# Local attention of a hybrid decoder step in plain fp32, on 64x64 and 128x64 tiles of the array

## The chip, the cores and the metric

The kernel runs on one core of one Trainium2 chip, as one launch. The metric is the device time of an execution in microseconds (us), as the median of several runs. The core's engines are named as the profile names them: PE (TensorE, matmuls; PEld is its weight load), DVE (VectorE), ACT (ScalarE), POOL (GpSimd) and SP (SyncE, which issues DMAs).

## What is computed

One layer of a decoder trunk for 1024 prompt tokens and 8 single-token samples. Ten projections of the normalised input feed two branches: retention (4 heads) and local attention (16 query heads of width 64 in 4 groups, one key/value head per group, a window of 128 keys, a learned sink per head). The branches are gated, projected, merged and projected once more. The change is in the local attention of the prompt alone, which is this part of the reference:

```python
def sink_attention(q, k, v, allowed, sinks):
    s = jnp.einsum('bnqhgd,bnkhd->bnhgqk', q.astype(jnp.float32), k.astype(jnp.float32)) * (SWA_HD ** -0.5)
    s = jnp.where(allowed[None, :, None, None], s, -jnp.inf)
    sink = jnp.broadcast_to(sinks.astype(jnp.float32)[None, None, :, :, None, None], s.shape[:-1] + (1,))
    p = jax.nn.softmax(jnp.concatenate([s, sink], axis=-1), axis=-1)[..., :-1]
    return jnp.einsum('bnhgqk,bnkhd->bnqhgd', p, v.astype(jnp.float32))

def swa_prompt(q, k, v, sinks):
    ...
    i = jnp.arange(SWA_BLOCK)[:, None]
    j = jnp.arange(2 * SWA_BLOCK)[None, :]
    d = i + SWA_BLOCK - j
    band = (d >= 0) & (d < WINDOW)
    ...
    o = sink_attention(qb, with_prev(kb), with_prev(vb), allowed, sinks)
```

A query at place i of a block of 128 sees keys i+1 to 127 of the block before and 0 to i of its own: 128 keys in all.

## The kernel before

**Stages.** Phase 1 first normalises and transposes the input. Then it goes through eight groups of work, four of retention and four of local attention (one per key/value head, `g`). The stretch from 416 to 900 us of the span holds the local attention. Phases 2 and 3, the projections of the branches and the output, follow. The large projections, lines 211 to 213 and 221 to 223, run in all stages. Each multiplies fp32 data that was split into a high and a low part of type fp32r, by three matmuls (high by high, high by low, low by high).

**One block of local attention** is `swa_tile(g, t)`, for t = 0 to 7, 32 in all; block 0 of a group has no block before it. It is a generator with five steps. First comes a projection to 384 columns (256 of queries for 4 heads, 64 of keys, 64 of values, `acc`), then the norm and rotary work on DVE, ACT and POOL. In step two, queries (`qr`, line 512) and keys (`kd`, line 513, the 64 columns twice) are transposed on PE. The queries are then stored as `qs` with the high part in partitions 0 to 63 and the low part in 64 to 127 (lines 517 and 518). The keys go into `kThi` and `kTlo`, each twice over the partitions. In step three, lines 533 and 534, each head has one matmul with `kThi` and one with `kTlo`, over 256 keys (128 in block 0). Since the weights `qs` hold both parts, two matmuls give the sum of all products. DVE then puts the keys of the block before over those that the mask forbids (line 536), takes the maximum (538), and ACT takes the exponential (487). So 128 probabilities per query are left, stored as in a ring. In step four the probabilities are transposed (545) and split into `pThi` and `pTlo` (lines 138 and 139), and four selects on POOL (554) make of them the part that belongs to the block before (`pHp`, `pLp`) and the part of the own block. In step five four matmuls (565, 566; two in block 0) of 512 columns, 4 heads of 128 queries, multiply these by values `vv`, high part in columns 0 to 63 and low in 64 to 127. Lines 568 and 572 add the two halves and store them in `oT`.

**Order.** `groups` writes a list of steps: a block's own next step, steps of the two blocks before it, and between them steps of gates and merge gates (`gate_block`, `mg_block`), which are projections and serve as filling. A scheduler of the framework then sets the order of instructions on each engine by a timeline of its own. Each engine runs its own list in order. Score tiles come from a pool of two PSUM buffers (`psc`), weighted sums from one (`pav`).

**Other fp32 matmuls of the kernel before.** Lines 442, 610 and 624 multiply plain fp32 data, without parts, on column tiles of the array that are 32 wide (`tile_position=(0, 32 * i)`). They serve the 8 samples. An fp32 matmul stands as two rows in the trace, an fp32r matmul as one.

Of the kernel before, what the change touches and what calls it, by code (L numbers as in the profile page):

```python
# [18 lines left out]
P = 128  # L19
D = 1024  # L20
SEQ = 1024
# [7 lines left out]
SH, KVH, G, HD = 16, 4, 4, 64  # L29
# [45 lines left out]
def shape_constants():  # L75
# [17 lines left out]
    i = np.arange(P)[:, None]  # L93
    j = np.arange(P)[None, :]
    out["c_band"] = (j > i) * 1.0
    misc = np.zeros((P, NMISC))
    for h in range(RH):
# [24 lines left out]
class Body:  # L122
# [370 lines left out]
    def swa_tile(self, g, t, units, st, oT):  # L493
        nc = self.nc
        acc = self.t(self.pacc, [P, 512], "acc")
        self.gemm_tok(acc[:, :384], units, self.hhi, self.hlo, t)
        qr, kd, rs = self.swa_rope(acc[:, :384], t)
        vv = self.t(self.ap, [P, 2, HD], "vv", F32R, bufs=4)
        self.copy_hi_lo(vv[:, 0, :], vv[:, 1, :], acc[:, 320:384], nc.vector)
        if t == NT - 1:  # L500
            vf = self.t(self.ap, [P, HD], "vf", bufs=1)
            nc.scalar.activation(out=vf[:], in_=acc[:, 320:384], func=AF.Copy)
            nc.sync.dma_start(out=self.o["kp"][0, 0, :, g, :], in_=kd[:, 0, :])
            nc.sync.dma_start(out=self.o["vp"][0, 0, :, g, :], in_=vf[:])
        vprev, st["v"] = st["v"], vv
        yield
        if t == 0:
            st["k"] = (self.t(self.ap, [P, SEQ], "kThi", F32R, bufs=1), self.t(self.ap, [P, SEQ], "kTlo", F32R, bufs=1))
# [12 lines left out]
        self.copy_hi_lo(khi[:, ks], klo[:, ks], pt[:, 2, :], nc.vector)  # L521
        yield
        k0 = (t - 1) * P if t else 0
        nk = 2 * P if t else P
        s = self.t(self.ap, [P, G, P], "s", bufs=2)
        mx = self.t(self.sm, [P, 4], "mx", bufs=2)
        two = lambda x: x.unsqueeze(1).broadcast_to([P, 2, P])
        scs = []
        for i in range(2):
            sc = self.t(self.psc, [P, 2, 256], "sc")  # L530
            for a in range(2):
                j = 2 * i + a
                nc.tensor.matmul(sc[:, a, :nk], qs[:, i, a, :], khi[:, k0 : k0 + nk], start=True, stop=False)  # L533
                nc.tensor.matmul(sc[:, a, :nk], qs[:, i, a, :], klo[:, k0 : k0 + nk], start=False, stop=True)  # L534
            cur = sc[:, :, nk - P : nk]
            nc.vector.copy_predicated(
                out=cur, mask=two(self.after[:].bitcast(U32)), data=sc[:, :, 0:P] if t else two(self.neg[:]))
            nc.vector.tensor_reduce(out=mx[:, 2 * i : 2 * i + 2], in_=cur, axis=AX.X, op=ALU.max)
            scs += [sc[:, a, nk - P : nk] for a in range(2)]
# [6 lines left out]
        big = lambda x: x[:].rearrange("p (j n) -> p j n", j=G)  # L546
        new = lambda nm: self.t(self.ap, [P, 512], nm, F32R, bufs=2 if "T" in nm else 1)
        hi, lo = new("pThi"), new("pTlo")
        self.copy_hi_lo(hi[:], lo[:], pt[:].rearrange("p a b -> p (a b)"), nc.vector)
        pT = [(hi, lo)]  # L550
        if t:
            hp, lp = new("pHp"), new("pLp")
            for dst, src, sign in ((hp, hi, 1), (lp, lo, 1), (hi, hi, -1), (lo, lo, -1)):
                nc.gpsimd.affine_select(
                    out=big(dst), in_=big(src).bitcast(F32), compare_op=ALU.is_ge, fill=0.0,
                    base=-1 if sign > 0 else 0, pattern=[[0, G], [-sign, P]], channel_multiplier=sign)
            hc, lc = hi, lo
            pT = [(hp, lp), (hc, lc)]
        nblk = len(pT)
        yield  # L560
        vs = [vprev, vv] if nblk == 2 else [vv]
        po = self.t(self.pav, [P, 512], "av")
        for blk in range(nblk):
            w = vs[blk][:].rearrange("p a b -> p (a b)")
            nc.tensor.matmul(po[:], w, pT[blk][0][:], start=(blk == 0), stop=False)  # L565
            nc.tensor.matmul(po[:], w, pT[blk][1][:], start=False, stop=(blk == nblk - 1))  # L566
        bot = self.t(self.ap, [HD, 512], "rbig", bufs=1)
        nc.scalar.activation(out=bot[:], in_=po[HD:P, :], func=AF.Copy)
        b4 = bot[:].rearrange("p (i a n) -> p i a n", i=2, a=2)
        p4 = po[0:HD, :].rearrange("p (i a n) -> p i a n", i=2, a=2)  # L570
        for a in range(2):
            nc.vector.tensor_tensor(out=oT[a * HD : (a + 1) * HD, :, ks], in0=p4[:, :, a, :], in1=b4[:, :, a, :], op=ALU.add)

    def swa_rows(self, g, units, oT):
        nc = self.nc
# [283 lines left out]
    def swa_consts(self):  # L859
# [6 lines left out]
        self.after = self.t(ap, [P, P], "band")  # L866
        nc.sync.dma_start(out=self.after[:], in_=self.i["c_band"][:])
        self.neg = self.t(ap, [P, P], "neg")
        nc.gpsimd.memset(self.neg[:], NEG)
        self.sink = self.t(ap, [P, SH], "sink")  # L870
        nc.sync.dma_start(out=self.sink[:], in_=self.i["swa_sinks"][0:1, :].broadcast_to([P, SH]))
        self.nsink = self.t(ap, [P, SH], "nsink")
# [135 lines left out]
```

## Time and profile before

| | us |
|---|---|
| runs | 1172.18, 1173.7, 1174.65 |
| median of the 3 runs | 1173.7 |
| the profiled execution, its own time | 1171.8 |
| span of its trace | 1170.0 |
| PE busy | 1148.1 |
| DVE busy | 638.6 |
| ACT busy | 436.8 |
| POOL busy | 428.3 |

The profile is one execution. Spans start at the core's first instruction. A matmul's duration in the trace overlaps that of the next one, so a row's cost is read as the distance from its start to the next row's start. A form such as 128*32 in a PE row gives the array's rows and columns that are used, and 128x256 the output's partitions or rows and columns.

### The profile page before, as it was taken

How to read it: one execution, taken by the hardware profiler on the slowest of the kernel's cores; microseconds unless marked ns; L12 is line 12 of the kernel's file. 1: busy time of each engine (PE TensorE's matmuls, PEld its weight loads, DVE VectorE, ACT ScalarE, POOL GpSimd, SP SyncE). 2: the span in 40 equal slices, each digit the busy share in tenths (PEclk: the TensorE clock that was granted, in tenths of full speed). 3: DMA queues.
4: the chain of work that ended last, by engine and by line, in shares of the span. 5: the costliest groups of instructions: out<-in, count | busy, mean ns of one | idle time of the engine just before them, and what ended most of it. 6: DMA issues, size and time to landing. Idle time of an engine off the chain costs nothing.

```text
span 1170.0 us, 19270 instructions
## 1 busy us (share of the span) xinstructions
PE 1148.1 (98%) x7140; PEld 1095.1 (94%) x7140; DVE 638.6 (55%) x1818; ACT 436.8 (37%) x1130; POOL 428.3 (37%) x398
## 2 busy tenths in 40 slices
PE   6999999999999999999999999999999999999998
PEld 5899999999999999999999999999999999999876
DVE  5854545555543487767766766678634312564121
ACT  6543342343344244544453455345534201221010
POOL 5434025216225435634463446345742211221010
PEclk9999999999999999999999999999999999999999
DMA  9224115314123411311141114102437744544221
GB/s 321 61 81 123 51 40 184 97 43 126 37 63 104 140 32 59 107 43 32 33 138 38 33 33 138 38 16 74 140 132 227 232 149 148 166 129 136 82 91 64
DMA packets 125165, 116.51 MB, mean 100 GB/s; under 512 B 17608, under 2 KB 113224, under 8 KB 125040
## 3 DMA queue, kind: packets, MB, share of 16 engines
q1 hardware_dynamic: 118160, 106.83, 29.6%
q10 hardware_dynamic: 6912, 8.46, 2.0%
q8 instruction: 56, 0.92, 0.3%
q14 instruction: 37, 0.30, 0.1%
HBM read 84.88 MB, written 32.44 MB: 100 GB/s over the span
## 4 chain that ended last, share of the span: by engine, by line
PE 90%; DVE 3%; DMA 2%; issue 2%; POOL 1%; ACT 1%; SPq 0%; ACTq 0%; POOLq 0%; DVEq 0%
PE acc L211 16%; PE acc L212 15%; PE acc L213 15%; PE acc L221 10%; PE acc L223 10%; PE acc L222 10%; PE acc L231 1%; PE acc L232 1%; PE sc L533 1%; PE sc L534 1%; PE av L565 1%; PE av L566 1%; PE tr L545 1%; DMA oT<-d_o 1%; POOL wlo L168 1%
## 5 line engine op out<-in xcount | busy, mean ns | idle before, releaser
L168 POOL TENSOR_TENSOR wlo<-wraw,whi 128x1024 fp32r<-128x1024 f32 (+1 forms) x92 | 205.5, 2240 | 303.7 <-ACT whi L167 260.4
L211 PE MATMUL acc<-hhi,whi 128*128 128x344 f32 x864 | 279.8, 324 | 1.5 <-ACT tg L297 1.5
L212 PE MATMUL acc<-hlo,whi 128*128 128x344 f32 x864 | 277.6, 321 | 0.0
L213 PE MATMUL acc<-hhi,wlo 128*128 128x344 f32 x864 | 277.3, 321 | 0.0
L221 PE MATMUL acc<-whi,hhi 128*128 128x384 f32 x512 | 175.5, 343 | 2.5 <-ACT hhi L138 1.2
L223 PE MATMUL acc<-whi,hlo 128*128 128x384 f32 x512 | 174.5, 341 | 0.0
L222 PE MATMUL acc<-wlo,hhi 128*128 128x384 f32 x512 | 174.5, 341 | 0.0
L211 PEld LDWEIGHTS acc<-hhi,whi 128*128 128x128 f32 x864 | 162.5, 188 | 4.6 <-ACT tg L297 2.2
L212 PEld LDWEIGHTS acc<-hlo,whi 128*128 128x128 f32 x864 | 162.4, 188 | 1.3
L213 PEld LDWEIGHTS acc<-hhi,wlo 128*128 128x128 f32 x864 | 162.4, 188 | 1.2 <-POOL wlo L168 0.2
L167 ACT ACTIVATE whi<-wraw 128x1024 fp32r<-128x1024 f32 (+1 forms) x92 | 90.3, 984 | 173.5 <-PE acc L212 110.0
L146 POOL TENSOR_TENSOR rs<-ms,nhalf 128x1 f32<-128x1 f32 (+3 forms) x81 | 68.5, 848 | 206.6 <-DVE ms L145 205.7
L221 PEld LDWEIGHTS acc<-whi,hhi 128*128 128x128 f32 x512 | 97.0, 190 | 4.8 <-ACT hhi L138 1.6
L222 PEld LDWEIGHTS acc<-wlo,hhi 128*128 128x128 f32 x512 | 97.0, 189 | 0.5 <-issue 0.2
L223 PEld LDWEIGHTS acc<-whi,hlo 128*128 128x128 f32 x512 | 96.9, 189 | 0.5 <-DVE hlo L139 0.2
L287 POOL TENSOR_TENSOR oT<-oT,tg 128x344 f32<-128x344 f32 x48 | 48.3, 1007 | 64.7 <-DVE tg L285 54.4
L487 ACT ACTIVATE s<-sc,ng,rs 128x128 f32<-128x128 f32 x128 | 56.9, 455 | 22.9 <-DVE ng L484 22.6
L223 PE MATMUL acc<-whi,mlo 128*128 128x512 f32 x128 | 50.5, 395 | 0.0
L222 PE MATMUL acc<-wlo,mhi 128*128 128x512 f32 x128 | 50.3, 393 | 0.0
L221 PE MATMUL acc<-whi,mhi 128*128 128x512 f32 x128 | 50.1, 393 | 0.0
L975 DVE TENSOR_TENSOR x<-acc,x 128x512 f32<-128x512 f32 x16 | 11.0, 690 | 68.7 <-PE acc L223 63.8
L285 DVE SCALAR_TENSOR_TENSOR tg<-tg,acc 128x344 f32<-128x344 f32 x48 | 24.5, 510 | 31.4 <-ACT tg L284 31.1
(361 smaller groups left out, 2372.9 us busy)
## 6 DMA issues: line engine op xcount, KB each, us to landing
wraw<-in_w_in SPq DMA_DIRECT2D x36, 512.0 KB
d_t<-tg ACTq DMA_DIRECT2D x48, 172.0 KB
d_o<-oT SPq DMA_DIRECT2D x16, 516.0 KB
tt<-d_t SPq DMA_DIRECT2D x48, 172.0 KB
wraw<-in_w_in SPq DMA_DIRECT2D x32, 256.0 KB
st<-d_o SPq DMA_DIRECT2D x9, 516.0 KB
d_m<-tt SPq DMA_DIRECT2D x24, 172.0 KB
mm<-d_m SPq DMA_DIRECT2D x24, 172.0 KB
```

The costliest lines, as they stand in the source:

```text
L146: nc.gpsimd.tensor_tensor(out=rs[:p, :width], in0=ms[:p, :width], in1=self.nhalf[:p, :width], op=ALU.pow)
L167: nc.scalar.activation(out=hi[:, :f], in_=raw[:, :f], func=AF.Copy)
L168: nc.gpsimd.tensor_tensor(out=lo[:, :f], in0=raw[:, :f], in1=hi[:, :f].bitcast(F32), op=ALU.subtract)
L211: nc.tensor.matmul(ps, whi[:, k, :], hi[:, cs], start=(k == 0), stop=False)
L212: nc.tensor.matmul(ps, whi[:, k, :], lo[:, cs], start=False, stop=False)
L213: nc.tensor.matmul(ps, wlo[:, k, :], hi[:, cs], start=False, stop=(k == KT - 1))
L221: nc.tensor.matmul(ps, hi[:, k, a:b], whi[:, kk, :], start=(k == 0), stop=False)
L222: nc.tensor.matmul(ps, hi[:, k, a:b], wlo[:, kk, :], start=False, stop=False)
L223: nc.tensor.matmul(ps, lo[:, k, a:b], whi[:, kk, :], start=False, stop=(k == KT - 1))
L285: nc.vector.scalar_tensor_tensor(out=tg[:], in0=tg[:], scalar=1.0, in1=ps[:, :BL], op0=ALU.add, op1=ALU.mult)
L287: nc.gpsimd.tensor_tensor(out=sl, in0=sl, in1=tg[:], op=ALU.mult)
L487: nc.scalar.activation(out=s[:p, j, :], in_=src[j], func=AF.Exp, bias=ng[:p, j : j + 1], scale=scale[j], accum_out=l[:p, j : j + 1])
```

## The change

The local attention of the prompt no longer splits its operands: queries, keys, probabilities and values stay fp32, and each product is one fp32 matmul. The scores are made in four 64x64 tiles of the array: two halves of its rows for two heads (`a`) by two halves of its columns for the two halves of the queries of a block (`e`). A half of 64 queries needs 192 keys (64 or 128 in block 0). The two heads' scores now stand in two PSUM tiles, each in a bank of its own. The mask shrinks to 64 columns. The probabilities are copied once (`pA`, on ACT). Four selects on POOL over 64 partitions and 256 elements zero one triangle in each half and write the other into `pB`, whose upper half stays zero. The weighted sums run in two column halves, on 128x64 tiles: `pA` with one order of the values and `pB` with the other. For that, POOL keeps a second copy of the values with the partition halves exchanged (`vv[:, 1]`). In block 0 both matmuls use the first column half and `pB` is not used.

```diff
@@ swa_tile
-        vv = self.t(self.ap, [P, 2, HD], "vv", F32R, bufs=4)
-        self.copy_hi_lo(vv[:, 0, :], vv[:, 1, :], acc[:, 320:384], nc.vector)
+        vv = self.t(self.ap, [P, 2, HD], "vv", bufs=4)
+        nc.scalar.activation(out=vv[:, 0, :], in_=acc[:, 320:384], func=AF.Copy)
+        for e in range(2):
+            nc.gpsimd.tensor_copy(out=vv[(1 - e) * HD : (2 - e) * HD, 1, :], in_=vv[e * HD : (e + 1) * HD, 0, :])
...
-        qs = self.t(self.ap, [P, 2, 2, P], "qs", F32R, bufs=2)
-        for a in range(2):
-            src = pt[a * HD : (a + 1) * HD, 0:2, :]
-            nc.scalar.activation(out=qs[0:HD, :, a, :], in_=src, func=AF.Copy)
-            nc.vector.tensor_tensor(out=qs[HD:P, :, a, :], in0=src, in1=qs[0:HD, :, a, :].bitcast(F32), op=ALU.subtract)
-        khi, klo = kT
+        qs = self.t(self.ap, [P, 2, P], "qs", bufs=2)
         ks = slice(t * P, (t + 1) * P)
-        self.copy_hi_lo(khi[:, ks], klo[:, ks], pt[:, 2, :], nc.vector)
+        nc.scalar.activation(out=qs[:], in_=pt[:, 0:2, :], func=AF.Copy)
+        nc.vector.tensor_copy(out=kT[:, ks], in_=pt[:, 2, :])
...
         for i in range(2):
-            sc = self.t(self.psc, [P, 2, 256], "sc")
             for a in range(2):
-                j = 2 * i + a
-                nc.tensor.matmul(sc[:, a, :nk], qs[:, i, a, :], khi[:, k0 : k0 + nk], start=True, stop=False)
-                nc.tensor.matmul(sc[:, a, :nk], qs[:, i, a, :], klo[:, k0 : k0 + nk], start=False, stop=True)
+                pa = slice(a * HD, (a + 1) * HD)
+                for e in range(2):
+                    k1 = t * P + (e + 1) * HD
+                    nc.tensor.matmul(
+                        sc[a][e * HD : (e + 1) * HD, i, lo[e] : 3 * HD], qs[pa, i, e * HD : (e + 1) * HD], kT[pa, k1 - 3 * HD + lo[e] : k1],
+                        start=True, stop=True, tile_position=(a * HD, e * HD))
...
-        hi, lo = new("pThi"), new("pTlo")
-        self.copy_hi_lo(hi[:], lo[:], pt[:].rearrange("p a b -> p (a b)"), nc.vector)
-        pT = [(hi, lo)]
+        pA = self.t(self.ap, [P, G, 2, HD], "pA", bufs=2)
+        nc.scalar.activation(out=pA[:].rearrange("p j e n -> p (j e n)"), in_=pt[:].rearrange("p a b -> p (a b)"), func=AF.Copy)
+        pB = self.pB[t % 2]
         if t:
...
+            for dst in (pB, pA):
+                for e in range(2):
+                    old = (dst is pA) == (e == 0)
+                    sign = 1 if old else -1
+                    nc.gpsimd.affine_select(
+                        out=dst[HD:P, :, e, :], in_=pA[HD:P, :, e, :], compare_op=ALU.is_ge, fill=0.0,
+                        base=-1 if old else 0, pattern=[[0, G], [-sign, HD]], channel_multiplier=sign)
         yield
...
-            nc.tensor.matmul(po[:], w, pT[blk][0][:], start=(blk == 0), stop=False)
-            nc.tensor.matmul(po[:], w, pT[blk][1][:], start=False, stop=(blk == nblk - 1))
...
+        po = self.t(self.pav, [P, 2, G, HD], "av")
+        for e in range(2):
+            natural, rolled = (lambda x: x[:, 0, :]), (lambda x: x[:, 1, :])
+            pick = natural if e else rolled
+            nc.tensor.matmul(po[0:HD, e], pick(vv if e or not t else vprev), pA[:, :, e, :], start=True, stop=True, tile_position=(0, 0))
+            if t:
+                nc.tensor.matmul(po[HD:P, e], pick(vprev if e else vv), pB[:, :, e, :], start=True, stop=True, tile_position=(0, HD))
```

The change also moves instructions, since the scheduler sets the order anew. On PE, the scores of a block in the middle of the local attention stood like this before, `qs` being the queries and `kThi`, `kTlo` the parts of the keys:

```order
L212 MATMUL acc_7493<-hlo_122,whi_7329 128x344
L533 MATMUL sc_7421<-kThi_6565,qs_7397 128x256
L534 MATMUL sc_7421<-kTlo_6566,qs_7397 128x256
L533 MATMUL sc_7421<-kThi_6565,qs_7397 128x256
L534 MATMUL sc_7421<-kTlo_6566,qs_7397 128x256
L213 MATMUL acc_7493<-hhi_121,wlo_7330 128x344
L221 MATMUL acc_7521<-whi_6049,hhi_121 128x384
L533 MATMUL sc_7428<-kThi_6565,qs_7397 128x256
L534 MATMUL sc_7428<-kTlo_6566,qs_7397 128x256
L533 MATMUL sc_7428<-kThi_6565,qs_7397 128x256
L534 MATMUL sc_7428<-kTlo_6566,qs_7397 128x256
L222 MATMUL acc_7521<-wlo_6050,hhi_121 128x384
```

And in the changed kernel, `kT` being the plain keys, x2 meaning two matmuls in a row:

```order
L211 MATMUL acc_7404<-hhi_121,whi_7247 128x344
L529 MATMUL sc_7332<-kT_6518,qs_7316 64x192 x2
L529 MATMUL sc_7333<-kT_6518,qs_7316 64x192 x2
L529 MATMUL sc_7332<-kT_6518,qs_7316 64x192 x2
L529 MATMUL sc_7333<-kT_6518,qs_7316 64x192 x2
L212 MATMUL acc_7404<-hlo_122,whi_7247 128x344
L213 MATMUL acc_7404<-hhi_121,wlo_7248 128x344
```

The eight score matmuls now stand in one run of eight, where two projections (lines 213 and 221) parted them. The runs are not always whole: over the 32 blocks the scores stand in 37 runs and the weighted sums in 33, and at nine places such a run, or one of the 32-wide tiles, borders directly on another.

The weighted sums of the same block, on PE, before; `pHp` and `pLp` are the probabilities of the block before, and each matmul is parted from the next by projections (the two of the own block, not shown, follow in the same way):

```order
L211 MATMUL acc_7713<-hhi_121,whi_7479 128x344
L565 MATMUL av_7668<-pHp_7603,vv_7050 128x512
L212 MATMUL acc_7713<-hlo_122,whi_7479 128x344
L213 MATMUL acc_7713<-hhi_121,wlo_7480 128x344
L211 MATMUL acc_7713<-hhi_121,whi_7479 128x344
L566 MATMUL av_7668<-pLp_7604,vv_7050 128x512
L212 MATMUL acc_7713<-hlo_122,whi_7479 128x344
L213 MATMUL acc_7713<-hhi_121,wlo_7480 128x344
L211 MATMUL acc_7741<-hhi_121,whi_7479 128x344
L565 MATMUL av_7668<-pThi_7599,vv_7232 128x512
L212 MATMUL acc_7741<-hlo_122,whi_7479 128x344
```

And in the changed kernel, line 565 being the first column half and line 567 the second:

```order
L212 MATMUL acc_7615<-hlo_122,whi_7390 128x344
L213 MATMUL acc_7615<-hhi_121,wlo_7391 128x344
L565 MATMUL av_7570<-pA_7505,vv_6982 64x256
L567 MATMUL av_7570<-pB_1171_4822,vv_7157 64x256
L565 MATMUL av_7570<-pA_7505,vv_7157 64x256
L567 MATMUL av_7570<-pB_1171_4822,vv_6982 64x256
L211 MATMUL acc_7615<-hhi_121,whi_7390 128x344
L212 MATMUL acc_7615<-hlo_122,whi_7390 128x344
```

Four weighted sums, each between projections, have become one run of four.

## Rows read from the trace of the kernel before

**Rows 1.** The page, parts 1 and 2: busy us, share, instructions; TensorE over 40 slices.

```profile
PE 1148.1 (98%) x7140; PEld 1095.1 (94%) x7140; DVE 638.6 (55%) x1818; ACT 436.8 (37%) x1130; POOL 428.3 (37%) x398
PE   6999999999999999999999999999999999999998
```

**Rows 2.** Busy us of each engine (instructions), granted clock, DMA: the local-attention stretch.

```profile
core 0: us, PE busy (x) PEld busy (x) DVE busy (x) ACT busy (x) POOL busy (x), PEclk, DMA share, GB/s
416.00:900.00 484.00, 481.05 (x3083) 464.90 (x3082) 327.19 (x1014) 228.88 (x645) 230.23 (x217) 1.00 0.25 77
```

**Rows 3.** Waits of TensorE, whole span: us in total, times, longest.

```profile
PE sc L533 <- ACT kThi L138: 0.9, 1, 0.9
PE tr L545 <- DVE s L491: 0.8, 1, 0.8
```

**Rows 4.** Groups of TensorE by line and shape: count, busy us, mean ns.

```profile
L533 PE MATMUL sc<-kThi,qs 128*128 128x256 f32 x112 | 27.7, 283 | 0.9 <-ACT kThi L138 0.9
L565 PE MATMUL av<-pThi,vv 128*128 128x512 f32 x32 | 12.8, 400 | 0.0
L565 PE MATMUL av<-pHp,vv 128*128 128x512 f32 x28 | 11.2, 399 | 0.0
```

**Rows 5.** Order of time, TensorE, score matmuls of one block: start us, us.

```profile
493.08 0.28 PE L534 MATMUL sc<-kTlo,qs 128*128 128x256 f32 x1
...
493.79 0.32 PE L213 MATMUL acc<-hhi,wlo 128*128 128x344 f32 x1
```

**Rows 6.** Order of time, TensorE, score matmuls of a first block.

```profile
526.98 0.28 PE L533 MATMUL sc<-kThi,qs 128*128 128x128 f32 x1
...
527.42 0.28 PE L534 MATMUL sc<-kTlo,qs 128*128 128x128 f32 x1
```

**Rows 7.** Order of time, TensorE, one weighted-sum matmul among projections.

```profile
580.75 0.40 PE L566 MATMUL av<-pLp,vv 128*128 128x512 f32 x1
580.99 0.33 PE L213 MATMUL acc<-hhi,wlo 128*128 128x344 f32 x1
```

**Rows 8.** Order of time, TensorE, four column tiles of 32, fp32, 128 columns.

```profile
535.11 0.32 PE L212 MATMUL acc<-hlo,whi 128*128 128x344 f32 x1
535.27 0.31 PE L213 MATMUL acc<-hhi,wlo 128*128 128x344 f32 x1
535.51 0.43 PE L610 MATMUL sc<-rbig,zq 128*32 128x128 f32 x8
535.87 0.45 PE L221 MATMUL acc<-whi,hhi 128*128 128x384 f32 x1
```

**Rows 9.** The same, 256 columns: four tiles at 87.53, two at 132.66.

```profile
87.53 0.64 PE L442 MATMUL av<-st,zq 128*32 128x256 f32 x8
88.10 0.38 PE L201 MATMUL sc<-vhi,phi 128*128 128x256 f32 x1
88.32 0.28 PE L202 MATMUL sc<-vlo,phi 128*128 128x256 f32 x1
...
132.66 0.63 PE L442 MATMUL av<-st,zq 128*32 128x256 f32 x4
133.22 0.33 PE L364 MATMUL tr<-ident,kr 128*128 128x128 f32 x1
```

**Rows 10.** Order of time, TensorE, a transpose that puts out 64 columns.

```profile
483.76 0.28 PE L630 MATMUL tr<-ident,osr 128*64 128x128 f32 x1
484.03 0.32 PE L213 MATMUL acc<-hhi,wlo 128*128 128x344 f32 x1
```

**Rows 11.** Groups of other engines by line and shape, 416 to 900 us.

```profile
L518 DVE TENSOR_TENSOR qs<-tr,qs 64x256 fp32r<-64x256 f32 x61 | 25.8, 422 | 9.4 <-ACT qs L517 7.6
L138 ACT ACTIVATE pThi<-tr 128x512 fp32r<-128x512 f32 x32 | 19.1, 597 | 18.6 <-PE tr L545 18.4
L168 POOL TENSOR_TENSOR wlo<-wraw,whi 128x1024 fp32r<-128x1024 f32 x27 | 65.0, 2410 | 74.0 <-ACT whi L167 74.0
L554 POOL TENSOR_SCALAR_AFFINE_SELECT pHp<-pThi 128x512 fp32r<-128x512 f32 x28 | 18.0, 642 | 33.6 <-ACT pThi L138 33.6
```

More of the change, by code (lines that the diff above doesn't have):

```diff
@@ L92, in shape_constants @@
     out["c_maskT"] = np.stack([(n >= m) * np.exp(-(m + 1.0) * lg[h]) * sc for h in range(RH)], 1)
-    i = np.arange(P)[:, None]
-    j = np.arange(P)[None, :]
+    i = np.arange(P)[:, None] % HD
+    j = np.arange(HD)[None, :]
     out["c_band"] = (j > i) * 1.0
@@ L497, in swa_tile @@
         qr, kd, rs = self.swa_rope(acc[:, :384], t)
-        vv = self.t(self.ap, [P, 2, HD], "vv", F32R, bufs=4)
-        self.copy_hi_lo(vv[:, 0, :], vv[:, 1, :], acc[:, 320:384], nc.vector)
+        vv = self.t(self.ap, [P, 2, HD], "vv", bufs=4)
+        nc.scalar.activation(out=vv[:, 0, :], in_=acc[:, 320:384], func=AF.Copy)
+        for e in range(2):
+            nc.gpsimd.tensor_copy(out=vv[(1 - e) * HD : (2 - e) * HD, 1, :], in_=vv[e * HD : (e + 1) * HD, 0, :])
         if t == NT - 1:
-            vf = self.t(self.ap, [P, HD], "vf", bufs=1)
-            nc.scalar.activation(out=vf[:], in_=acc[:, 320:384], func=AF.Copy)
             nc.sync.dma_start(out=self.o["kp"][0, 0, :, g, :], in_=kd[:, 0, :])
-            nc.sync.dma_start(out=self.o["vp"][0, 0, :, g, :], in_=vf[:])
+            nc.sync.dma_start(out=self.o["vp"][0, 0, :, g, :], in_=vv[:, 0, :])
         vprev, st["v"] = st["v"], vv
@@ L528, in swa_tile @@
-        scs = []
+        two = lambda x: x.unsqueeze(1).broadcast_to([x.shape[0], 2, HD])
+        lo = [0, 0] if t else [2 * HD, HD]
+        sc = [self.t(self.psc, [P, 2, 256], "sc") for a in range(2)]
         for i in range(2):
-            sc = self.t(self.psc, [P, 2, 256], "sc")
             for a in range(2):
-                j = 2 * i + a
-                nc.tensor.matmul(sc[:, a, :nk], qs[:, i, a, :], khi[:, k0 : k0 + nk], start=True, stop=False)
-                nc.tensor.matmul(sc[:, a, :nk], qs[:, i, a, :], klo[:, k0 : k0 + nk], start=False, stop=True)
-            cur = sc[:, :, nk - P : nk]
-            nc.vector.copy_predicated(
-                out=cur, mask=two(self.after[:].bitcast(U32)), data=sc[:, :, 0:P] if t else two(self.neg[:]))
-            nc.vector.tensor_reduce(out=mx[:, 2 * i : 2 * i + 2], in_=cur, axis=AX.X, op=ALU.max)
-            scs += [sc[:, a, nk - P : nk] for a in range(2)]
+                pa = slice(a * HD, (a + 1) * HD)
[4 more added lines that the diff above has]
+                        start=True, stop=True, tile_position=(a * HD, e * HD))
@@ new lines, in swa_tile @@
+        scs = [None] * G
+        for a in range(2):
+            if t == 0:
+                nc.vector.tensor_copy(out=sc[a][0:HD, :, HD : 2 * HD], in_=two(self.neg[0:HD]))
+            nc.vector.copy_predicated(
+                out=sc[a][:, :, 2 * HD : 3 * HD], mask=two(self.after[:].bitcast(U32)),
+                data=sc[a][:, :, 0:HD] if t else two(self.neg[:]))
+            cur = sc[a][:, :, HD : 3 * HD]
+            nc.vector.tensor_reduce(out=mx[:].rearrange("p (i a) -> p a i", a=2)[:, a], in_=cur, axis=AX.X, op=ALU.max)
+            for i in range(2):
+                scs[2 * i + a] = cur[:, i, :]
@@ L545, in swa_tile @@
             nc.tensor.transpose(out=pt[:, j, :], in_=s[:, j, :], identity=self.ident[:])
-        big = lambda x: x[:].rearrange("p (j n) -> p j n", j=G)
-        new = lambda nm: self.t(self.ap, [P, 512], nm, F32R, bufs=2 if "T" in nm else 1)
-        hi, lo = new("pThi"), new("pTlo")
-        self.copy_hi_lo(hi[:], lo[:], pt[:].rearrange("p a b -> p (a b)"), nc.vector)
-        pT = [(hi, lo)]
-        if t:
[L552 to L558, printed above, removed]
@@ L559, in swa_tile @@
-        nblk = len(pT)
-        yield
[L561 to L564, printed above, removed]
-            nc.tensor.matmul(po[:], w, pT[blk][0][:], start=(blk == 0), stop=False)
-            nc.tensor.matmul(po[:], w, pT[blk][1][:], start=False, stop=(blk == nblk - 1))
-        bot = self.t(self.ap, [HD, 512], "rbig", bufs=1)
-        nc.scalar.activation(out=bot[:], in_=po[HD:P, :], func=AF.Copy)
@@ L574, in swa_rows @@
+        if t:
+            bot = self.t(self.ap, [HD, 2, G, HD], "rbig", bufs=1)
+            nc.scalar.activation(out=bot[:], in_=po[HD:P], func=AF.Copy)
+        for a in range(2):
+            dst = oT[a * HD : (a + 1) * HD, :, ks].rearrange("p i (e n) -> p i e n", e=2)
+            if t:
+                nc.vector.tensor_tensor(out=dst, in0=view(po[0:HD], a), in1=view(bot[:], a), op=ALU.add)
+            else:
+                nc.vector.tensor_copy(out=dst, in_=view(po[0:HD], a))
     def swa_rows(self, g, units, oT):
@@ L865, in swa_consts @@
         nc.vector.tensor_scalar(out=self.rng[:], in0=self.rng[:], scalar1=0.5, scalar2=None, op0=ALU.mult)
-        self.after = self.t(ap, [P, P], "band")
+        self.after = self.t(ap, [P, HD], "band")
         nc.sync.dma_start(out=self.after[:], in_=self.i["c_band"][:])
-        self.neg = self.t(ap, [P, P], "neg")
+        self.neg = self.t(ap, [P, HD], "neg")
         nc.gpsimd.memset(self.neg[:], NEG)
+        self.pB = [self.t(ap, [P, G, 2, HD], f"pB{i}") for i in range(2)]
+        for x in self.pB:
+            nc.gpsimd.memset(x[0:HD], 0.0)
         self.sink = self.t(ap, [P, SH], "sink")
```

9 lines of the change are left out of this document (2 added, 7 removed).

## The prediction

> **What bounds the kernel now.** I read the page's busy lines and slices first. TensorE is busy for 98% of the span, and from the second of 40 slices on every slice but the last shows a 9 [rows 1]. Then I read the stretch of the local attention: TensorE is busy for 481.05 of 484.00 us at a granted clock of 1.00, which is the level of 2.4 GHz. DVE, ACT and POOL are busy for 327, 229 and 230 us [rows 2]. Then the waits. In the steps that the change touches, TensorE waited for scores' operands 0.9 us and for probabilities 0.8 us, once each [rows 3]. So in this stretch the time is the sum of what the matmuls cost TensorE. What DVE, ACT and POOL save or add is worth nothing until TensorE waits for it.
>
> Since rows of matmuls overlap, I take a matmul's cost as the distance to the next start. Seen so, six score matmuls between 493.08 and 493.79 cost 0.118 us each [rows 5], those of a first block 0.11 (four between 526.98 and 527.42) [rows 6], and a weighted sum 0.235 (580.75 to 580.99, 0.23 elsewhere) [rows 7].
>
> **What is removed.** There are 32 blocks, 28 of them with a block before it: the 112 rows of one part are 28 times 4 heads, and one sum has 28 rows [rows 4]. Each of the 28 loses 8 score matmuls (8 x 0.118 = 0.95) and 4 weighted sums (4 x 0.235 = 0.94), each of the 4 first blocks 8 x 0.11 = 0.88 and 2 x 0.235 = 0.47. Together that is 28 x 1.89 + 4 x 1.35 = 58.3 us of TensorE.
>
> **What is added, and its price.** No row of before shows an array tile of 64 columns or 64 rows in fp32. The nearest are the four column tiles of 32 that multiply fp32 for the samples. Four matmuls stand as eight rows, two passes each. With 128 columns they take 0.36 us (535.51 to 535.87) [rows 8], with 256 columns 0.57 (87.53 to 88.10) [rows 9]. So 128 columns more in each of two passes cost 0.21, which is 0.83 ns per column and pass. Two tiles in place of four cost 0.56 (132.66 to 133.22) [rows 9], so the tiles stream abreast. Of the 0.36 us, 2 x 128 x 0.83 ns = 0.21 is streaming and 0.15 is not. Two more costs lie around such a run. The projection before it takes 0.24 us to the next start where the one before that took 0.16 [rows 8], so 0.08. The matmul behind it takes 0.22 (88.10 to 88.32) [rows 9] where its like costs 0.118 [rows 5], so 0.10. One excursion to tiles and back therefore costs about 0.34 us beside its streaming.
>
> Scores: each of the four 64x64 tiles has two matmuls of 192 columns, four passes, so 4 x 192 x 0.83 ns = 0.64 us if the four stream abreast, and 0.98 with the excursion, against 0.95 before. In a first block the longer tile has 4 x 128 x 0.83 ns = 0.43, so 0.77 against 0.88. Weighted sums: each column half has two matmuls of 256 columns, so 4 x 256 x 0.83 ns = 0.85, and 1.19 against 0.94. In a first block both matmuls lie in the same column half, so that nothing is abreast: 1.19 against 0.47.
>
> That makes 28 x (0.03 + 0.25) = 7.8 and 4 x (0.72 - 0.11) = 2.4. The order of the changed kernel adds to it. The 32 blocks have 37 runs of scores and 33 of weighted sums, six more than needed, at 0.34 each: 2.0. Three of the split blocks put the two upper tiles in one run and the two lower in another, which streams 0.64 twice, and two split off a remainder of about 0.32: 2.6. Nine runs border on another run of tiles, where I take off half an excursion each, 1.5. The sum is +13.3 us, all on TensorE and so on the path.
>
> **What the other engines do.** The four low parts on DVE go: `qs` alone was 61 rows of 0.42 us [rows 11] in this stretch. ACT keeps a copy of the probabilities (0.60), and POOL keeps four selects, of 64x256 instead of 128x512 (0.64) [rows 11]. I cost the saving at nothing: it is hidden behind TensorE's 481 us. If that cover were gone, at most TensorE's idle 3.0 us [rows 2] could be won. POOL's two new copies of the values are queued behind the block's norm and ahead of selects of older blocks. The weighted sums need them two steps later, some 25 us, so I cost them at nothing too.
>
> **New waits.** The scores of a block now ask for both score tiles at once, but a block's next scores come a block later, about 13 us. The way from the transposed probabilities to the weighted sums is tighter. Priced by the distances above, the order of after leaves 5.0 us of TensorE's work in the median there and 3.3 at the least, where before had 5.4 and 4.1. The copy takes 0.60. A select lies between 0.32 (half the elements) and 0.64 us (no faster at all). So the chain is 0.6 + 4 x 0.32 to 4 x 0.64 = 1.9 to 3.2 us, to which the last transpose's own 0.27 comes. That just fits, unless a 2.41 us split of weights [rows 11] stands in front on POOL, whose list is in order. I take 0, with 5 to 10 us as the upper end.
>
> **Two rules of the Trainium skill.** The rows show column tiles abreast, but none shows tiles that differ in rows. The Trainium skill, "TensorE: Matmul & The Clock Gate" (Part 3, measured speedup), says that four row tiles ran 3.07 times as fast as one after another. An estimate by that page, 4/3.07 on the scores' 0.64, would add 28 x 0.19 = 5 us. The sum keeps the rows' 0.64.
> The rows also show 0.34 us per excursion. The Trainium skill, "TensorEngine Tiling (Array Packing)" (Key Properties), says that a change of tiling mode drains the engine, and gives no time. By that rule the cost falls on 64-wide tiles as well and the sum stands; without it the third rival below holds.
>
> **The rivals.**
> *Row halves not abreast.* If the upper and the lower two 64x64 tiles take turns, 25 blocks pay another 0.64 and the first blocks another 0.43: +17.7, so +31. For it speaks that no row shows them abreast; against it that column tiles run so, and that the two halves write different banks.
> *A wait for the probabilities takes the place of the low parts.* If selects stand behind a split of weights in a third of the 28 blocks, at about 0.5 to 1 us each, the sum becomes +18 to +23. Against it: before had hardly more room and TensorE waited for no weighted sum.
> *No cost to enter and leave 64-wide tiles: faster.* The streaming alone is 28 x 1.49 + 4 x 1.28 + 2.6 = 49.5 us, under the 58.3 removed. The point from which it decides is 0.13 us per excursion (8.8 over 70). At nothing, it is -9. For it: a transpose that puts out 64 columns cost only 0.27 together with the projection behind it (483.76 to 484.03) [rows 10], of which the projection alone is 0.16 [rows 8]. Against it: every run of 32-wide tiles paid about 0.3, and that transpose may use the whole array.
> That the change doesn't do what it says is ruled out by the order, which shows all matmuls of the parts gone.
>
> **How the numbers follow.** The profiled execution took 1171.8 us, of which 1170.0 are the span. It is 1.9 under the median of 1173.7, so the sum goes on the median: 1173.7 + 13.3 = 1187. Chances: the forecast 0.60, from 1181 to 1193 (an excursion from 0.25 to 0.42 us, idle time by 3). Row halves in turn 0.16, at 1202 to 1210, around 1205. The wait 0.12, at 1191 to 1197. No cost to enter 0.12, at 1163 to 1172. From 1179 to 1206 lies all of the forecast and of the wait and half of the first rival, some 8 in 10. About 0.2% (2.3 us) is what a measurement of this kernel can tell from no change, as its runs lie 2.5 us apart. Faster by more is 0.10, from the last rival; within it 0.04, from its upper end; slower 0.86.
>
> **What would show it.** In the trace after: sixteen rows of a block's scores from first to last start in some 0.5 us, and about 0.8 to the next matmul (right), or some 1.2 and 1.4 (rows in turn). Eight rows of weighted sums with about 1.0 to the next start. A matmul behind such a run at 0.10 above its like. DVE's busy time lower by some 70 us with no gain in time. The prediction is wrong if the 64-wide tiles are entered for nothing, if the row halves take turns, or if TensorE's waits name POOL or ACT at the weighted sums.

## The result and the profile after

The changed kernel takes 1185.07 us in the median (1183.40 to 1185.07, but for one execution of 6457.74), against 1173.85 (1172.18 to 1174.65) before: 11.2 us more, a ratio of 1.0092 with an interval of 1.0074 to 1.0110. The profiled execution took 1185.06 us, of which its span is 1183.3.

First the page of the changed kernel, its busy lines and two of the rows of slices. They answer to [rows 1].

```profile
PE 1162.9 (98%) x7516; PEld 1074.6 (91%) x7516; DVE 577.4 (49%) x1698; ACT 412.8 (35%) x1058; POOL 416.5 (35%) x464
...
PE   5999999999999999999999999999999999999998
...
PEclk9899999999999999999999999999999999999999
```

Then the stretch of the local attention, as in [rows 2]: length, busy time and count of PE, PEld, DVE, ACT and POOL, the granted clock, the share of DMA and GB/s.

```profile
416.00:900.00 484.00, 483.06 (x3388) 432.60 (x3387) 263.96 (x902) 202.59 (x573) 213.45 (x274) 1.00 0.24 73
```

DVE lost 63 us of work here, ACT 26 and POOL 17. TensorE's idle time went from 2.95 to 0.94 us. So the other engines were relieved by over 100 us, and of that no more than the 2.0 us by which TensorE's idle time fell turned into time.

All of TensorE's waits in this stretch are one row (engine, operation and line, who ended the wait, us in total, times, longest), where [rows 3] had two of 0.9 and 0.8 in the steps of the change:

```profile
PE tr L548 <- DVE s L491: 0.9, 1, 0.9
```

No row names a weighted sum or a score. What is left is the price of the matmuls. The scores of a block, in order of time (start, duration, engine, line, tiles, array rows and columns, shape, count):

```profile
449.25 0.32 PE L211 MATMUL acc<-hhi,whi 128*128 128x344 f32 x1
449.50 0.89 PE L529 MATMUL sc<-kT,qs 64*64 64x192 f32 x16
450.31 0.42 PE L212 MATMUL acc<-hlo,whi 128*128 128x344 f32 x1
450.57 0.32 PE L213 MATMUL acc<-hhi,wlo 128*128 128x344 f32 x1
450.73 0.32 PE L211 MATMUL acc<-hhi,whi 128*128 128x344 f32 x1
```

From start to start, the projection ahead takes 0.25 where its like takes 0.16 (450.57 to 450.73). The sixteen rows of the scores take 0.81, and the projection behind them 0.26. So a block's scores cost 0.09 + 0.81 + 0.10 = 1.00 us (1.01 where a block's run is whole, in the mean), of which 0.64 is the streaming of the prediction and 0.36 is not. A block's weighted sums:

```profile
453.33 0.33 PE L222 MATMUL acc<-wlo,hhi 128*128 128x384 f32 x1
453.50 0.33 PE L223 MATMUL acc<-whi,hlo 128*128 128x384 f32 x1
453.76 0.43 PE L565 MATMUL av<-pA,vv 128*64 128x256 f32 x1
453.77 0.43 PE L567 MATMUL av<-pB,vv 128*64 128x256 f32 x1
454.03 0.38 PE L565 MATMUL av<-pA,vv 128*64 128x256 f32 x1
...
454.78 0.45 PE L221 MATMUL acc<-whi,hhi 128*128 128x384 f32 x1
455.06 0.33 PE L222 MATMUL acc<-wlo,hhi 128*128 128x384 f32 x1
```

The two column halves start 0.01 us apart and stream abreast. With 0.26 ahead (0.17 for its like, 453.33 to 453.50), 1.02 for the eight rows and 0.28 behind, they cost 0.09 + 1.02 + 0.11 = 1.22 here, 1.21 in the mean of 24 such runs, against four times 0.235 before [rows 7].

To see where the 11.2 us lie, I summed the distance from each TensorE row to the next over all that starts after 300 us of the span, once for each kernel. These distances hold TensorE's idle time, 4.7 us before and 2.7 after; 0.9 of the 4.7 lie behind one old weighted sum:

| rows of TensorE, from 300 us to the last | before, us | after, us | difference |
|---|---|---|---|
| scores | 30.25 | 28.37 | -1.9 |
| weighted sums | 29.7 | 32.6 | +2.9 |
| projections of 344 columns, 3000 rows in both | 482.9 | 489.3 | +6.4 |
| projections of 384 columns, 947 and 960 rows | 169.3 | 174.6 | +5.3 |
| transposes of step two and four | 19.9 | 20.5 | +0.6 |
| everything there is | 865.6 | 879.2 | +13.6 |

Without idle time everything grew by 15.6 us, and the matmuls of the change themselves by 1.9 together. The rest sits in the projections beside them, whose number did not change in the program: each row ahead of a run of tiles and each row behind it is longer. The 13 extra rows of 384 columns are another matter. They mean that the execution after was 13 x 0.177 = 2.3 us behind at 300 us already. The windows at 45 us show why, first of before, then of after (columns as above):

```profile
45.00:50.00 5.00, 4.09 (x27) 3.48 (x28) 2.92 (x12) 1.54 (x7) 1.01 (x2) 1.00 0.04 14
50.00:55.00 5.00, 5.00 (x33) 4.50 (x32) 3.26 (x12) 2.77 (x8) 0.00 (x0) 1.00 0.00 0
```

```profile
45.00:50.00 5.00, 4.47 (x19) 3.31 (x20) 2.68 (x12) 1.65 (x7) 0.81 (x2) 0.51 0.02 5
50.00:55.00 5.00, 5.00 (x28) 4.54 (x27) 1.30 (x5) 1.24 (x4) 0.00 (x0) 0.81 0.00 0
```

In the profiled execution of after the granted clock stood at 0.51 there, which is the level of 1.2 GHz, before local attention had begun; TensorE had been busy for 3.36 of the 5.00 us ahead of it, and in the execution of before, whose clock did not fall, for 3.62. I do not put it down to the change: other executions of the kernel before have mean clocks of 0.996 to 0.999 as well, though no trace shows where in them it was lower. So of the 13.3 us between the two spans 2.3 belong to the clock, and about 11 to the change, as in the medians.

### The profile page after: what moved, and what is told of

It is laid out like the page before. It is cut to its first block, busy times and chain, and to the rows that moved or that the text cites. A ratio compares the mean times of both kernels' runs of the same rounds, so it can differ in the third digit from the quotient of the medians.

```text
span 1183.3 us, 19971 instructions
## 1 busy us (share of the span) xinstructions
PE 1162.9 (98%) x7516; PEld 1074.6 (91%) x7516; DVE 577.4 (49%) x1698; ACT 412.8 (35%) x1058; POOL 416.5 (35%) x464
## 4 chain that ended last, share of the span: by engine, by line
PE 94%; DMA 2%; DVE 2%; issue 1%; POOL 1%; ACT 0%; SPq 0%; POOLq 0%; ACTq 0%; DVEq 0%
PE acc L211 17%; PE acc L212 16%; PE acc L213 16%; PE acc L223 10%; PE acc L221 10%; PE acc L222 10%; PE av L565 3%; PE sc L529 2%; PE acc L232 1%; PE acc L231 1%; PE tr L548 1%; PE tr L338 1%; DMA wraw<-in_w_br_ret 1%; PE sc L201 1%; PE sc L203 1%
## 5 line engine op out<-in xcount | busy, mean ns | idle before, releaser
L211 PE MATMUL acc<-hhi,whi 128*128 128x344 f32 x864 | 283.5, 328 | 0.6 <-ACT tg L297 0.6
L287 POOL TENSOR_TENSOR oT<-oT,tg 128x344 f32<-128x344 f32 x48 | 45.7, 951 | 63.4 <-DVE tg L285 59.4
```

The source lines that it names most:

```text
L211: nc.tensor.matmul(ps, whi[:, k, :], hi[:, cs], start=(k == 0), stop=False)
L287: nc.gpsimd.tensor_tensor(out=sl, in0=sl, in1=tg[:], op=ALU.mult)
```

## The experiments

My theory was the one of the prediction: TensorE bounds the stretch, each run of fp32 tiles costs its streaming, with all tiles abreast, plus about 0.34 us to enter and leave, and what the other engines save is worth nothing.

**The scores alone.** New scores, old weighted sums.

```diff
-        vv = self.t(self.ap, [P, 2, HD], "vv", bufs=4)
+        vv = self.t(self.ap, [P, 2, HD], "vv", F32R, bufs=4)
...
-        pA = self.t(self.ap, [P, G, 2, HD], "pA", bufs=2)
+        hi, lo = new("pThi"), new("pTlo")
...
+            nc.tensor.matmul(po[:], w, pT[blk][0][:], start=(blk == 0), stop=False)
+            nc.tensor.matmul(po[:], w, pT[blk][1][:], start=False, stop=(blk == nblk - 1))
```

> The new scores (fp32, four 64x64 tiles) with the old weighted sums in high and low parts. The old sums take the probabilities in another order of keys, so the local attention's output is not the reference's; the amount of work is that of the old sums. Theory (a sum of prices on TensorE, 0.97 us for a block's scores in place of 0.95, most of the loss in the sums): 28 x 0.02 - 4 x 0.1, and 11 runs of scores more than 32 in this order at 0.34 each, less eight shared borders: +2 to +4, so 1176 to 1178. Rival (the 64x64 tiles are what costs, not the sums): 1182 to 1185.

Measured: 1180.57 us, a ratio of 1.0054 (1.0041 to 1.0067), 6.8 us more than before. My theory fell short here by 3 to 5 us, and the reason is the order. In this kernel the scheduler cuts the scores of 32 blocks into 43 runs, where the changed kernel has 37. One such cut:

```profile
446.43 0.87 PE L529 MATMUL sc<-kT,qs 64*64 64x192 f32 x8
447.23 0.43 PE L211 MATMUL acc<-hhi,whi 128*128 128x344 f32 x1
...
449.92 0.87 PE L529 MATMUL sc<-kT,qs 64*64 64x192 f32 x8
450.71 0.44 PE L221 MATMUL acc<-whi,hhi 128*128 128x384 f32 x1
```

Half of the block's tiles take 0.80 us and the other half 0.79, each as long as all four together (0.81 above), because each half streams all its columns. A cut through the middle of a block thus costs the whole streaming again and another entry, about 1 us. Four blocks are cut so, others into a large and a small part. My expectation had counted the 43 runs at the price of an entry each, but left out that the parts stream again, which the sum of the prediction has. The rows of the scores take 31.2 us here, where 32 whole runs would take 28 x 0.81 + 4 x 0.60 = 25.1. Of these 6.1 us more, 11 x 0.17 = 1.9 are the fixed part inside each run (0.81 less 0.64), and some 4 are columns streamed again.

**The weighted sums alone.** Old scores, new weighted sums.

```diff
-        qs = self.t(self.ap, [P, 2, P], "qs", bufs=2)
+        qs = self.t(self.ap, [P, 2, 2, P], "qs", F32R, bufs=2)
...
+                nc.tensor.matmul(sc[:, a, :nk], qs[:, i, a, :], khi[:, k0 : k0 + nk], start=True, stop=False)
+                nc.tensor.matmul(sc[:, a, :nk], qs[:, i, a, :], klo[:, k0 : k0 + nk], start=False, stop=True)
```

> The old scores in high and low parts with the new weighted sums (fp32, two column halves). The order of keys differs again, so the local attention's output is not the reference's. Theory: 28 x (1.21 - 0.94) + 4 x (1.20 - 0.47) + 4 runs more at 0.34 = +11.8, so about 1185, the whole of the change's loss. Rival (the scores' tiles cost it): 1174 to 1177.

Measured: 1182.13 us, 1.0072 (1.0058 to 1.0086), 8.4 us more. The clock was 1.00 in both profiled executions, so their spans can be compared: 1177.8 to 1170.0, 7.8 us. By the trace the distances after 300 us, idle time apart, grew by 10.6 us. The window explains the difference:

```profile
416.00:900.00 484.00, 483.58 (x3151) 448.95 (x3151) 305.24 (x950) 225.30 (x637) 220.71 (x275) 1.00 0.24 75
```

TensorE is idle for 0.42 us where it was idle for 2.95 [rows 2]. The price is there; 2.5 us of old idle time paid for part of it. Both halves of the change lose by themselves. By the prices the weighted sums lose more; the two times, 6.8 and 8.4 us, do not show that, since their intervals overlap and each kernel has an order of its own.

**Both column halves in the first blocks too.**

```diff
-            nc.tensor.matmul(po[0:HD, e], pick(vv if e or not t else vprev), pA[:, :, e, :], start=True, stop=True, tile_position=(0, 0))
+            ce = 0 if t else e * HD
+            nc.tensor.matmul(po[ce : ce + HD, e], pick(vv if e or not t else vprev), pA[:, :, e, :], start=True, stop=True, tile_position=(0, ce))
...
```

> The changed kernel, but in the first block of each group the two weighted sums take one column half each in place of both the first. Theory (abreast in place of one after the other): 4 x 0.43 = 1.7 less than the changed kernel, so 1183.3. Rival (column halves in fp32 gain nothing abreast): 1185, as the changed kernel.

Measured: 1184.55 us, 1.0092 (1.0079 to 1.0106), 0.5 less than the changed kernel, which the time cannot tell from nothing. The trace can. First the changed kernel, then this one, a first block's weighted sums:

```profile
432.44 1.08 PE L565 MATMUL av<-pA,vv 128*64 128x256 f32 x4
433.45 0.66 PE L608 MATMUL tr<-ident,kc 128*128 128x128 f32 x4
```

```profile
432.37 0.65 PE L566 MATMUL av<-pA,vv 128*64 128x256 f32 x4
432.95 0.66 PE L610 MATMUL tr<-ident,kc 128*128 128x128 f32 x4
```

The run fell from 1.01 to 0.58 us in each of the four blocks, so 1.7 us in all. It was lost again elsewhere: TensorE is idle 1.70 us in the stretch instead of 0.94, and one more block has its scores cut through the middle (five runs of eight rows stand alone instead of three), about 0.9. So the local gain is shown, and idle time and the order took it.

**The low parts' work on DVE put back**, with nobody waiting for it.

```diff
+        idle = self.t(self.ap, [P, 512], "idle", bufs=1)
+        nc.vector.tensor_tensor(out=idle[:], in0=pt[:].rearrange("p a b -> p (a b)"), in1=pA[:].rearrange("p j e n -> p (j e n)"), op=ALU.subtract)
```

(the same for queries and keys.)

> The changed kernel with DVE work put back that nobody reads: per block two subtractions of 64x256, one of 128x128 and one of 128x512, some 60 us in all, as much as the change took from DVE. Theory (the relief of DVE is worth nothing while TensorE is busy): as the changed kernel, 1185 within 2. Rival (the relief paid for part of the loss): 1188 to 1195.

Measured: 1185.87 us, 1.0100 (1.0086 to 1.0113).

```profile
416.00:900.00 484.00, 482.86 (x3380) 431.78 (x3379) 331.44 (x1026) 202.05 (x573) 212.94 (x274) 1.00 0.24 73
```

DVE is back at 331 us, over its 327 of before, and the time moved by 0.8, inside the runs' spread. DVE's relief is worth nothing, as expected.

**Two excursions instead of one.** Between the two halves of a block's weighted sums stands a transposition on the whole array, so that TensorE leaves the tiles and comes back.

```diff
...
+            if e == 0:
+                with self.tc.issue_after(m.ins):
+                    nc.tensor.transpose(out=po[:, 1, 0:2, :].rearrange("p j n -> p (j n)"), in_=pA[:, 0:1].rearrange("p j e n -> p (j e n)"), identity=self.ident[:])
```

> The changed kernel with a 128x128 transpose on the whole array between the two halves of each block's weighted sums (32 of them; what it writes is written over). Theory (each entry into tiles and back costs 0.34 us, the transpose 0.11): 32 x 0.45 = 14.4 more than the changed kernel, about 1199. Rival (the 0.34 is no price of entering tiles, and the transpose alone is paid): 32 x 0.11 = 3.5 more, about 1189.

Measured: 1196.66 us, 1.0198 (1.0182 to 1.0213), 11.6 us over the changed kernel, 0.36 per block. In the trace:

```profile
442.43 0.32 PE L211 MATMUL acc<-hhi,whi 128*128 128x344 f32 x1
442.68 0.43 PE L565 MATMUL av<-pA,vv 128*64 128x256 f32 x1
...
443.27 0.33 PE L571 MATMUL av<-ident,pA 128*128 128x128 f32 x1
443.52 0.43 PE L565 MATMUL av<-pA,vv 128*64 128x256 f32 x1
...
444.11 0.42 PE L212 MATMUL acc<-hlo,whi 128*128 128x344 f32 x1
444.37 0.32 PE L213 MATMUL acc<-hhi,wlo 128*128 128x344 f32 x1
```

From 442.43 to 444.37 are 1.94 us; without the two projections' own 0.32, 1.62, against 1.21 for the run in one piece: 0.41 for excursion and transposition together. I had expected 0.34 + 0.11 = 0.45. Of this, 0.36 shows in the time, in part because TensorE's last 0.9 us of idle time in the stretch went with it. How the 0.41 divides between the two is not shown. The rival of no cost to enter and leave is refuted. Another rival is that the price belongs to the change between fp32r and fp32 and not to the tiles. Most of it does not: the transposition's operands are plain fp32 like those of the tiles, and leaving the tiles for it and coming back still cost 0.30 beside the 0.11 that a transposition takes among projections (0.27 less 0.16 in [rows 10]). A plain fp32 product on the whole array was not run.

**Only one half of the array's rows.** The heads of the lower half use the upper half's operands, so that the same columns stream through two tiles instead of four.

```diff
-                pa = slice(a * HD, (a + 1) * HD)
+                pa = slice(0, HD)
...
-                        start=True, stop=True, tile_position=(a * HD, e * HD))
+                        start=True, stop=True, tile_position=(0, e * HD))
```

> The changed kernel with all score matmuls on the upper row half of the array: 64x64 tiles in two column halves, each with twice the passes. Heads 1 and 3 of a group use the queries of heads 0 and 2, so the output is not the reference's; the number and size of the matmuls is the same. Theory (four tiles stream abreast in the changed kernel): 28 x 0.64 + 4 x 0.43 = 19.6 more, about 1205. Rival (the row halves take turns in the changed kernel anyway): 1185.

Measured: 1201.79 us, 1.0239 (1.0225 to 1.0253), 16.7 over the changed kernel.

```profile
451.20 0.32 PE L211 MATMUL acc<-hhi,whi 128*128 128x344 f32 x1
451.46 1.57 PE L529 MATMUL sc<-kT,qs 64*64 64x192 f32 x16
452.95 0.43 PE L212 MATMUL acc<-hlo,whi 128*128 128x344 f32 x1
```

The sixteen rows take 1.49 us in this run and 1.45 in the 22 others of their kind, instead of 0.81. The difference of 0.64 is the streaming. So the row halves are abreast in the changed kernel. The 19.6 us of my expectation counted all 28 blocks, but the three that are cut between the row halves already stream twice: 25 x 0.64 + 4 x 0.43 = 17.7. The rows of the scores take 46.0 us instead of 28.4, which is that.

**Runs that are not cut.** The matmuls of one block's scores, and of its weighted sums, in a section that nothing can enter.

```diff
+        with self.tc.tile_critical():
...
                     nc.tensor.matmul(
...
+        with self.tc.tile_critical():
...
                 nc.tensor.matmul(po[0:HD, e], pick(vv if e or not t else vprev), pA[:, :, e, :], start=True, stop=True, tile_position=(0, 0))
```

> The changed kernel with the matmuls of a block's scores kept together as one run, and those of its weighted sums as well: 32 runs of scores and 32 of sums where the changed kernel has 37 and 33. The way of keeping them together puts two branches around each run on TensorE's list, 128 in all, which the changed kernel does not have. Theory (a split of a run costs another excursion of 0.34 us, and where the two upper tiles stand apart from the two lower, another 0.64 us of streaming): by the distances of the changed kernel's trace the splits cost 3 x 0.83 + 0.65 + 0.38 + 0.36 = 3.9 us, shared borders give back 0.5, so 3.4 us less: 1181.7 us, if the branches are free. Rival (a split costs nothing, since the scheduler only fills time that is idle anyway): 1185 us. Each branch that costs 0.02 us adds 2.6 us to either.

Measured: 1230.21 us, 1.0483 (1.0466 to 1.0500). It tells nothing of the cuts, because the sections cost more than all else:

```profile
450.07 0.32 PE L212 MATMUL acc<-hlo,whi 128*128 128x344 f32 x1
450.22 0.32 PE L213 MATMUL acc<-hhi,wlo 128*128 128x344 f32 x1
450.98 0.43 PE L567 MATMUL av<-pA,vv 128*64 128x256 f32 x1 [0.44 <-POOL oT L287]
```

The row before the run takes 0.76 from start to start, where it takes 0.25 in the changed kernel. 45 us over 64 runs are 0.70 per run. TensorE is idle for 40 us in the stretch, most of it ahead of the runs, and the trace names many different engines for these gaps; that the two branches are what costs it is not shown. What a kernel with whole runs and without branches would take was not tried.

**The other way to save columns.** The idea of 192 keys per half does not need fp32 tiles. This kernel keeps the high and low parts and the whole array, packs the 64 keys of the second block's high and low parts into one operand, and so replaces four weighted-sum matmuls of 512 columns by six of 256: against before, 28 x (0.94 - 6 x 0.118) = 6.5 us less of TensorE.

```diff
+        vlow = self.t(self.ap, [P, 2, HD], "vlow", F32R, bufs=3)
+        up = self.t(self.ap, [P, 2, HD], "vup", F32R, bufs=4)
+        for dst, r in ((vlow, 0), (up, HD)):
+            for b in (0, HD):
+                nc.gpsimd.tensor_copy(out=dst[b : b + HD], in_=vv[r : r + HD].bitcast(F32))
...
+            for e in range(2):
+                w = flat(vv if e else vprev)
+                nc.tensor.matmul(pv[:, :, e, :], w, hv[:, :, e, :], start=True, stop=False)
+                nc.tensor.matmul(pv[:, :, e, :], w, lv[:, :, e, :], start=False, stop=False)
+                nc.tensor.matmul(pv[:, :, e, :], flat(vup) if e else flat(vlow), pX[:, :, e, :], start=False, stop=True)
```

> The kernel before, in high and low parts on the whole array, with one thing of the change: a half of 64 queries needs 192 keys. The 64 rows of probabilities that are not in the main product are stacked, high part in one half of the rows and low part in the other, so that they need one matmul. A block's sums are then six matmuls of 256 columns in place of four of 512: 6 x 0.119 = 0.71 against 0.94 us. Theory: 28 x 0.23 = 6.4 less than before, about 1167. Rival (POOL's eight selects of 64x256 and four copies of values become a wait of TensorE): 1172 to 1180.

Measured: 1177.56 us, 1.0033 (1.0020 to 1.0045): slower than before, though TensorE has less to do. Its two long waits in the stretch, and the stretch itself:

```profile
PE acc L211 <- ACT tg L297: 5.1, 1, 5.1
PE sc L539 <- ACT kThi L138: 4.2, 1, 4.2
```

```profile
416.00:900.00 484.00, 473.92 (x3109) 463.13 (x3108) 332.00 (x1018) 227.14 (x646) 293.30 (x445) 0.99 0.25 76
```

TensorE is idle for 10.1 us, and POOL went from 230 [rows 2] to 293. Ahead of the second wait, which ends at 820.99, POOL's list reads:

```profile
807.68 0.89 POOL L565 TENSOR_SCALAR_AFFINE_SELECT pX<-pThi 64x256 fp32r<-64x256 f32 x2 [2.78 <-ACT pThi L138]
...
810.56 2.40 POOL L168 TENSOR_TENSOR wlo<-wraw,whi 128x1024 fp32r<-128x1024 f32 x1
...
815.14 4.94 POOL L168 TENSOR_TENSOR wlo<-wraw,whi 128x1024 fp32r<-128x1024 f32 x2
```

Splits of weights stand among the selects and close behind them, and POOL has no gap from 807.68 to 821. The first wait, of 5.1 us, ends at 892.17. Behind it the granted clock fell, to 0.50, the level of 1.2 GHz, from 890 to 895 us, and so to 0.70 in the mean of these 10 us (columns as above):

```profile
890.00:900.00 10.00, 7.83 (x39) 7.83 (x40) 3.82 (x3) 4.34 (x5) 2.52 (x1) 0.70 0.68 221
```

So idle time is not the whole of the loss: matmuls at the lower clock are part of it. The next kernel moves the four copies per block from POOL to ACT, and nothing else.

```diff
-                nc.gpsimd.tensor_copy(out=dst[b : b + HD], in_=vv[r : r + HD].bitcast(F32))
+                nc.scalar.activation(out=dst[b : b + HD], in_=vv[r : r + HD].bitcast(F32), func=AF.Copy)
```

> The packed form of the kernel before (hi and lo parts kept, 192 keys per weighted sum, six matmuls of 256 columns) with the four copies of the values per block on ACT instead of POOL, so that POOL does about what it did in the kernel before. Theory (the packed form lost its 28 x 0.235 = 6.6 us because POOL's 293 us in the stretch delayed the splits of weights and the norms): POOL falls to 230 +- 10 us in the stretch, the 4.2 us wait before a block's scores goes, and the time is 1168 to 1173. Rival (the gain is given back at the end of the stretch, where TensorE waits for attention outputs that come back by transfers): last weighted sum some 4 us earlier than before, but the first output projection not earlier than 888 us, and the time is 1173 to 1178.

Measured: 1169.68 us against 1174.17 before, a ratio of 0.9963 (0.9948 to 0.9977). This is faster than both kernels, and inside the theory's range. Its waits for scores (one more, of 0.5, is for a gate), and the stretch:

```profile
PE sc L539 <- ACT kThi L138: 2.3, 2, 1.9
PE sc L540 <- DVE kTlo L139: 1.1, 2, 0.8
```

```profile
416.00:900.00 484.00, 480.00 (x3166) 468.60 (x3165) 334.09 (x1025) 266.14 (x770) 255.42 (x330) 1.00 0.25 79
```

POOL is at 255, not at the 230 of the theory, and TensorE still waits 3.4 us for scores. Both long waits are gone, and with them most of the loss: 4.5 us of the 6.5 arrive. That the copies on POOL caused the waits is shown by taking them off POOL alone (with the order that the scheduler then sets). Through which of POOL's instructions the wait came is not shown.

## Why the prediction was right, step by step

The prediction said 1187.0, in the range 1179 to 1206, and slower. The time is 1185.07.

| term of the sum | predicted, us | read from the traces, us |
|---|---|---|
| scores of a block in one run | 0.98 | 1.01 |
| scores of a first block | 0.77 | 0.80 |
| weighted sums of a block in one run | 1.19 | 1.21 |
| weighted sums of a first block | 1.19 | 1.20 |
| what a shared border of two runs saves | 0.17 | 0.20 |
| all runs of the new tiles together | 71.6 | 72.8 |
| removed | 58.3 | 59.0 |
| idle time of TensorE in the stretch | 0 | -2.0 |
| the sum | +13.3 | +11.8 |

The row of all runs is what the tile runs of after cost (85.3, by distances as above), less the 12.5 of the runs of 32-wide tiles that were there before.

**The excursion** held. It came from 32-wide tiles, and the 64-wide ones pay the same, 0.36 against 0.34. Of the 0.36, 0.09 lie on the row ahead, 0.17 inside the run and 0.10 on the row behind, as the prediction had 0.08, 0.15 and 0.10. The Trainium skill, "TensorEngine Tiling (Array Packing)" (Key Properties), says that a change of tiling mode drains the engine; the runs agree in so far as one more excursion, with a transposition in it, cost 0.41 us per block.

**Tiles abreast** held, for columns and for rows. A run of a block's scores takes 0.81 us with both row halves and 1.45 with one. By the Trainium skill, "TensorE: Matmul & The Clock Gate" (Part 3, measured speedup), I had estimated 0.19 us per block for row tiles not quite abreast; of that the trace shows at most the 0.03 by which a block's scores exceed the forecast.

**No new wait** held. TensorE's waits name neither POOL nor ACT at the weighted sums.

**The relief of the other engines** was costed at nothing. For DVE the experiment with its work put back confirms it. But idle time fell by 2.0 us, of the 3.0 that I had named as the most. That term was mis-sized at zero. Idle stayed at 1.1 us with DVE's work put back, so it was not DVE's load that had made it; which of the moved instructions did is open.

**What is removed** was mis-sized by 0.7 us. The distances behind the old scores and weighted sums add up to 30.2 + 29.7 = 59.9, but 0.9 of it is no cost of a matmul. It is a wait of a projection for a gate, right behind one of the old weighted sums, and stands in the row of idle time already:

```profile
L211 PE MATMUL acc<-hhi,whi 128*128 128x344 f32 x521 | 168.4, 323 | 0.9 <-ACT tg L297 0.9
```

Without it a weighted sum took 0.240 in the mean, against the 0.235 of the one that I read.

**The size of the sum**: it is some 2 us too high (the medians say 11.2, the rows of the table 11.8), and that is the idle time, put at nothing. Without idle time the distances after 300 us grew by 15.6, of which 2.3 are the 13 rows of the lower clock, so by 13.3, just the sum. That it fits so well is in part luck: the runs cost 1.2 more than forecast, what they replaced 0.7 more, and the rest is spread over rows beside the old matmuls. That the two spans differ by just the predicted 13.3 is chance: 2.3 of it is the lower clock at 45 us in the profiled execution of after.

**The order's term** (six runs more than needed, and the streaming of cut blocks) was read from the order and is in the 72.8. The kernel with only the scores changed shows how much hangs on it. There six more runs go with 4.0 us more than the scores seem to cost in the changed kernel (6.8, against 11.2 - 8.4 = 2.8). The trace has the same: 2.8 us more on the rows of the scores themselves (31.2 against 28.4), and about 0.2 beside each of the six runs.

## What to carry to other kernels

Where TensorE bounds a stretch, count columns and excursions: a run of fp32 tiles cost 0.83 ns here per column and pass of its longest tile, plus 0.36 us to enter and leave, with two rows in it as with sixteen. So put as many matmuls as possible into one run, and look in the order for runs that are cut through the middle of a set of tiles, which stream twice. Packing rows and columns on the whole array has no excursion; check then which other engine's list has to carry the packing.

## What the runs showed that I had not expected

The 0.17 us that a run of scores pays inside lie on its first and last pass: from pass to pass it took 0.21, 0.16 and 0.16 us, and 0.28 from the last to the projection behind.

Two runs of different tiles that touch each other save less than a whole excursion, as I had guessed without a row for it: scores and then weighted sums took 2.02 us (the projections' own distances taken off) instead of 1.01 + 1.21. So the border between two tile forms still costs about half of an excursion, though both are fp32.

A select on POOL over 64 partitions and 256 elements took 0.44 us, where one over 128 and 512 took 0.64 [rows 11]: a quarter of the elements at two thirds of the time.

A section that nothing may enter cost TensorE about 0.7 us each; what in it costs that is not shown.
